# A decoder layer on one core: which engine makes a weight block's low part, where the gates' exponentials stay, and how the compression's places are read

## The chip, the core and the metric

The kernel runs on one core of a Trainium2 chip. The metric is the device time of one execution in microseconds (us), the median of the runs shown. The engines run side by side, each through its own queue of instructions in a fixed order, and wait for one another by semaphores: TensorE (PE) for matmuls, VectorE (DVE), ScalarE (ACT) and GpSimd (POOL) for elementwise work, SyncE (SP) for starting transfers from memory.

## The reference, cut to what matters

One layer: a convolution module and a sparse attention with three branches stand side by side, are gated and projected; then cross-attention; then a feed-forward block. x is 256 tokens by 1024. Three places of it are touched by the change:

```
z = blocks + pos;  z = einsum("bnlgd,lde->bnge", z, w1);  k_cmp = silu(z) @ w2     # 15 blocks of 32 tokens, 4 groups
g = sigmoid(gate_logits)                       # 256 tokens x 3 branches x 16 heads
o = g[0] * o_cmp + g[1] * o_slc + g[2] * o_win
y = sigmoid(g_conv) * conv_out + sigmoid(g_attn) * nsa_out     # g_attn = h @ 1024 columns of w_in
```

All is float32. A softmax follows each branch's scores, so a branch gate can be multiplied into its softmax's divisor.

## The kernel before, in words

**Split products.** A product of float32 matrices is made as three fast products: each operand is split into a rounded high part and a low part, the rest. `split` makes the two parts of a weight: ACT copies to the high part (L177), and a subtraction makes the low part (L179), on POOL for the blocks in the list `aside`, on DVE for all others. A block holds 256 columns of a weight and comes in two halves of 128x1024 values; `ga2_0` is the first half of the block ga2, `ga2_0h` and `ga2_0l` its parts. PE then makes high times high, high times low, low times high (L246).

**The blocks' order and buffers.** `CHUNKS` lists the blocks: ... vs, vw, ga0 to ga3 (the attention gate's logits), gc0 to gc3 (the convolution gate's), and so on. Before the change `aside` runs from u1 to ga1, so the low parts of ga0 and ga1 are made on POOL, those of ga2, ga3 and all later blocks on DVE. A half is loaded by SP (L210) into one of four buffers (tag "w"), free again when its low part is made; the high and low parts have five buffers each. The framework's scheduler plays the program against modelled times, fixes each engine's order by it and hands out each buffer that it holds to be free first; which load follows which subtraction is therefore part of the built program.

**The convolution's taps.** 31 taps per channel block are added up: on DVE by multiply-adds that accumulate in PSUM (`taps_v`, L422; the last of a chain writes to `yt`), and for the first block in part by ACT products (vw, L431) that POOL adds one after another to `yt` (`taps_g`, L434). Each of POOL's additions needs the result of the one before.

**The attention's start.** `compressed_scores` has PE make the compressed branch's scores into two banks (cs_ps0, cs_ps1); DVE adds them to the bias in `nsc` (L698). A first bank of tag "s" (two banks in all) is free for another use when that is done. The raw branch gates are transposed by PE to `gt_ps`, in the only bank of tag "s0". ACT writes exp(-g) of them to `sgt` in SBUF (L715), and DVE makes from that twice 1 + exp(-g) in two instructions, `igc` and `igd` (L718), which later divide the softmaxes. Then come the scores of the first pair of heads: `s1` (L735), one bank of tag "s" per head, and `s0` (L737) in the bank that gt_ps had. So the second s1 waits for nsc, and s0 for what reads gt_ps last. `between` makes the products of ga2, ga3, gc0 and so on in pieces between the pairs of heads.

**The compression.** `hidden` multiplies the gathered places of keys and values (`kvt`, per place 4 groups and one more for the position, each of 16) by `w1t` in 32 matmuls. Each reads 5 rows of 15 places, 75 columns with a step from row to row.

Of the kernel before, what the change touches and what calls it, by code (L numbers as in the profile page):

```python
# [11 lines left out]
AF = mybir.ActivationFunctionType  # L12
ALU = mybir.AluOpType
AX = mybir.AxisListType

P = 128
# [4 lines left out]
GROUPS = 4  # L21
HD = 64
# [8 lines left out]
NCMP = 15  # L31
# [4 lines left out]
CHUNKS = (  # L36
    [f"k{j}" for j in range(1, 4)] + [f"u{j}" for j in range(8)]
    + ["kc", "vc"] + [f"q{j}" for j in range(4)] + ["ks", "kw", "vs", "vw"]
    + [f"ga{j}" for j in range(4)] + [f"gc{j}" for j in range(4)]
    + [f"pw{j}" for j in range(4)] + [f"wo{j}" for j in range(4)]  # L40
    + [f"xq{j}" for j in range(4)] + [f"v{j}" for j in range(4)]
    + [f"xo{j}" for j in range(4)] + [f"f{j}" for j in range(NF)]
)
CHUNK_AT = {n: i for i, n in enumerate(CHUNKS)}
# [53 lines left out]
def tile_hybrid_block(  # L98
# [16 lines left out]
    nc = tc.nc  # L115
# [6 lines left out]
    def long(name, slot, shape=(P, NB, S), dt=F32):  # L122

        return sb.tile(list(shape), dt, tag=f"L{slot}", name=name)
# [9 lines left out]
    def small(name, shape, dt=F32, tag=None, bufs=1):  # L134
        if len(shape) == 2 and shape[1] < LINE:
            return sb.tile([P, LINE], dt, tag=tag or name, name=name, bufs=bufs)[:, 0:shape[1]]
        return sb.tile(shape, dt, tag=tag or name, name=name, bufs=bufs)
# [10 lines left out]
    def aux(name, shape, tag, bufs):  # L148
        return axp.tile(shape, F32, tag=tag, name=name, bufs=bufs)
# [31 lines left out]


    first, splits = {}, {}
    aside = CHUNKS[CHUNK_AT["u1"]:CHUNK_AT["ga2"]]

    def behind(*marks):

        stack = ExitStack()
        for m in marks:
            stack.enter_context(tc.issue_after(m.ins))  # L190
        return stack
# [40 lines left out]
    def in_line():  # L232
        return behind(*last)
# [153 lines left out]
    for i in range(4):  # L387
        hs = slice(2 * i, 2 * i + 2)
        for kb in (2 * i, 2 * i + 1):
            vec = nc.vector.scalar_tensor_tensor(out=hf[:, kb], in0=xt_t[:, kb], scalar=col(PP_GMIX, kb),  # L390
                                                 in1=r1, op0=ALU.mult, op1=ALU.mult)
# [62 lines left out]
    for j in range(NB):  # L454
        ps = gemm(f"u{j}", h)
        sg = small(f"sg{j}", [P, S], tag="sg", bufs=3)
# [9 lines left out]
    with behind(loads["u6_1"]):  # L466
# [5 lines left out]
                     start=True, stop=True)  # L472
    cb_ps = aux("cb_ps", [P, 2, 16, HEADS], "o", 1)
    for qb in range(2):
        for i, ns in enumerate(CGROUPS):
            n0, n1 = ns[0], ns[-1] + 1
            mm = nc.tensor.matmul(cb_ps[:, qb, n0:n1].rearrange("p n h -> p (n h)"), lhsT=cbt[:, i, qb * P:qb * P + P],
                                  rhs=relt[:, RT_CB + 16 * n0:RT_CB + 16 * n1], start=True, stop=True)
# [21 lines left out]
    kvt = [long(f"{n}t", slot, (P, 8, GROUPS + 1, 16)) for n, slot in (("k", 11), ("v", 13))]  # L500
    for kv, name in enumerate(("kc", "vc")):
        ps = gemm(name, h)
        kc = kvt[kv]
        for g in range(2):
            for odd in range(2):
                at = ps[HD * g:HD * g + HD].rearrange("p b (m l o) -> p b l m o", l=8, o=2)[:, :, :, :, odd]
# [10 lines left out]
    def hidden():  # L517


        z_ps = aux("z_ps", [P, GROUPS + 1, NCMP], "o", 1)  # L520
        with in_line():
            for l in range(16):
                for kv in range(2):
                    mm = nc.tensor.matmul(z_ps[HD * kv:HD * kv + HD], lhsT=w1t[:, kv, l],
                                          rhs=kvt[kv][:, l % 8, :, l // 8:l // 8 + NCMP], start=l == 0, stop=l == 15)
        last[:] = [mm]
        zs = small("zs", [P, GROUPS, NCMP], tag="zs", bufs=2)
        at = small("at", [P, 1])
        nc.scalar.activation(at, z_ps[:, GROUPS, 0:1], AF.Copy)
        sig = nc.scalar.activation(zs, z_ps[:, :GROUPS], AF.Sigmoid, bias=at)  # L530

        with behind(sig):
            nc.scalar.activation(small("exps", [P, 1]), eps1, AF.Exp)
        z1 = zz[:HD, 0, :64].rearrange("p (g n) -> p g n", g=GROUPS)[:, :, 0:NCMP]
        nc.vector.scalar_tensor_tensor(out=z1, in0=z_ps[:HD, :GROUPS], scalar=at[:HD], in1=zs[:HD], op0=ALU.add, op1=ALU.mult)
        nc.vector.scalar_tensor_tensor(out=zs[HD:], in0=z_ps[HD:, :GROUPS], scalar=at[HD:], in1=zs[HD:], op0=ALU.add, op1=ALU.mult)
        nc.scalar.activation(zz[HD:, 1].rearrange("p (g r n) -> p g r n", g=GROUPS, r=4)[:, :, :, 0:NCMP],
                             zs[HD:].unsqueeze(2).to_broadcast([HD, GROUPS, 4, NCMP]), AF.Copy)

# [17 lines left out]
    for j in range(4):  # L557
        ps = gemm(f"q{j}", h)
        q0, q1 = (qt[j // 2][:, 4 * (j % 2) + k:4 * (j % 2) + k + 3:2] for k in range(2))
        nc.scalar.activation(q0[0:64], ps[0:64], AF.Copy, scale=-0.125)  # L560
        act = nc.scalar.activation(q1[64:128], ps[64:128], AF.Copy, scale=-0.125)
        nc.vector.scalar_tensor_tensor(out=q0[64:128], in0=ps[0:64], scalar=-0.125, in1=f(q0[0:64]),
                                       op0=ALU.mult, op1=ALU.subtract)
        vec = nc.vector.scalar_tensor_tensor(out=q1[0:64], in0=ps[64:128], scalar=-0.125, in1=f(q1[64:128]),
                                             op0=ALU.mult, op1=ALU.subtract)
        convolve(11, (1, 0, 1, 1)[j], act, vec)
        if j == 1:
            hidden()
# [28 lines left out]
    ng = 3 * HEADS  # L597
# [9 lines left out]
    with in_line():  # L607
        for n, x in enumerate(h):
            for kb in range(NB):
                mm = nc.tensor.matmul(g_ps, lhsT=wgs[:, kb].rearrange("p c n -> p (c n)"), rhs=x[:, kb],  # L610
                                      start=n + kb == 0, stop=n * kb == NB - 1)
# [64 lines left out]
    with behind(splits["ga0_1"][1]):  # L676
        for c in range(2):
            for i in range(2):
                nc.gpsimd.tensor_tensor(out=vcm[:, c, 8 * i:8 * i + 8], in0=f(vcs[:, c, i]).unsqueeze(1).to_broadcast([P, 8, HD]),
                                        in1=hm, op=ALU.mult)  # L680
# [28 lines left out]
    gt_ps = aux("gt_ps", [P, 2, ng], "s0", 1)  # L709
# [1 line left out]
    for tb in range(2):  # L711
        nc.tensor.matmul(gt_ps[:, tb], lhsT=sgn[:, tb * P:tb * P + P], rhs=cpt[:, CP_GS:CP_GS + ng], start=tb == 0, stop=tb == 1)

    sgt = small("sgt", [P, 2, ng], tag="sg", bufs=3)
    nc.scalar.activation(sgt, gt_ps, AF.Exp, scale=-1.0)  # L715
    for to, g in ((igc, sgt[:, :, 0:HEADS]), (igd.rearrange("p h t b -> p t b h"),
                                              sgt[:, :, HEADS:3 * HEADS].rearrange("p t (b h) -> p t b h", b=2))):
# [6 lines left out]
    def scores(hp):  # L724

        g = hp // 2
        nbp = bias_of(hp)
        s0 = aux(f"s0_{hp}", [P, 2, 2, P], "s0", 1)
        p0 = small(f"p0_{hp}", [P, 2, 2, P], tag="p0", bufs=2)
        p1 = []  # L730
        for k, hd in enumerate(heads_of(hp)):
            s1 = aux(f"s1_{hd}", [P, 2, S], "s", 2)
            with in_line():
                for i, t in enumerate((kdh, kdl)):
                    nc.tensor.matmul(s1, lhsT=qh(hd, 1), rhs=t[:, g].rearrange("p b t -> p (b t)"), start=i == 0, stop=i == 1)  # L735
                for i, t in enumerate((kdh, kdl)):
                    mm = nc.tensor.matmul(s0[:, k], lhsT=qh(hd, 0), rhs=t[:, g, :, 0:P], start=i == 0, stop=i == 1)  # L737
            p1.append(small(f"p1_{hd}", [P, 2, S], tag="pr", bufs=4))
            for br in range(2):
                nc.vector.tensor_tensor_reduce(out=p1[k][:, br], in0=s1[:, br], in1=nbp[:, k], scale=1.0, scalar=3e38,  # L740
                                               op0=ALU.add, op1=ALU.min, accum_out=mins[:, hd, 1, br:br + 1])
        last[:] = [mm]
        for k, hd in enumerate(heads_of(hp)):
            for br in range(2):
                least = nc.vector.tensor_tensor_reduce(out=p0[:, k, br], in0=s0[:, k, br], in1=nbp[:, k, P:S], scale=1.0, scalar=3e38,
                                               op0=ALU.add, op1=ALU.min, accum_out=mins[:, hd, 0, br:br + 1])
        first["scores"] = least,
        return p0, p1
# [86 lines left out]
    p = [scores(0)]  # L835
# [462 lines left out]
    u1, u25, u3, u35 = more = [small(f"more{n}", [P, 512], tag="vt", bufs=4) for n in range(4)]  # L1298
# [187 lines left out]
```

## Time and profile before

| what | value |
|---|---|
| median of the runs shown | 539.82 us (3 runs, 539.81 to 545.05) |
| profiled execution, its own time | 542.99 us |
| span in its trace, first to last instruction | 540.7 us |
| mean granted TensorE clock | 0.992 |

The trace is of one execution with the profiler on; times in it count from the span's start. In its rows the engine stands before line, operation, out<-in and shape; tile names are without their numbers, so ga_0l can be the first half's low part of any of the four blocks. An idle time before an instruction stands in brackets with what ended it.

### The profile page before, as it was taken

The page shows a single profiled execution, that of the slowest core. Times are in us where ns is not written, and L with a number is a line of the kernel's source. Part 1 is how long each engine was busy: PE and PEld are TensorE (multiplying, and loading weights), DVE is VectorE, ACT ScalarE, POOL GpSimd, SP SyncE. Part 2 cuts the span into 40 slices and gives each one's busy share as a digit, 9 for nine tenths or more (in the row PEclk, how much of TensorE's full clock was granted, in tenths as well). Part 3 has the DMA queues.
Part 4 walks back from the last instruction along what each step waited for, and adds up shares of the span by engine and source line. Part 5 has one row for each costly group of instructions (what it writes and reads, how often), then busy time and mean ns, then how long its engine had stood idle before and what let it go on. Part 6 is the DMA issues. An engine that isn't in the chain of part 4 may idle for free.

```text
span 540.7 us, 10518 instructions
## 1 busy us (share of the span) xinstructions
PE 529.8 (98%) x3963; PEld 495.4 (92%) x3963; DVE 455.0 (84%) x913; ACT 357.6 (66%) x649; POOL 155.7 (29%) x109
## 2 busy tenths in 40 slices
PE   9999999999979999999999999999999999999995
PEld 8999999999969988999999999988888888888884
DVE  4868899899989898885869676588899999879996
ACT  4675475787674887969547755576676677648563
POOL 0079999899971000301003100150000000000001
PEclk9999999999979999999999999999999999999999
DMA  8927954665153744438655742757846668438632
GB/s 323 402 83 233 369 180 162 208 195 161 62 183 126 223 151 135 135 98 233 205 198 170 270 138 98 220 171 205 261 158 193 198 208 237 159 121 245 198 118 78
DMA packets 30739, 101.52 MB, mean 188 GB/s; under 512 B 3296, under 2 KB 5856, under 8 KB 30304
## 3 DMA queue, kind: packets, MB, share of 16 engines
q1 hardware_dynamic: 29104, 96.99, 53.8%
q0 software_dynamic: 864, 2.62, 2.8%
q10 hardware_dynamic: 720, 1.23, 0.6%
q8 instruction: 31, 0.51, 0.4%
q14 instruction: 20, 0.16, 0.1%
HBM read 99.59 MB, written 1.25 MB: 186 GB/s over the span
## 4 chain that ended last, share of the span: by engine, by line
PE 60%; DVE 1%; ACT 0%; issue 0%; ACTq 0%; DVEq 0%
PE ps_f L1203 15%; PE ps_f L1205 7%; PE fo L1242 6%; PE ps_xo L246 4%; PE ps_v L246 4%; PE ps_pw L246 4%; PE ps_wo L246 4%; PE ps_xq L246 4%; PE m L1242 4%; PE xo_ps L970 1%; PE xs L970 1%; PE o L801 1%; PE pt_a L780 1%; PE s L735 1%; PE o L798 1%; PE pt_b L780 0%
## 5 line engine op out<-in xcount | busy, mean ns | idle before, releaser
L422 DVE SCALAR_TENSOR_TENSOR yp<-vt,ppt,yp 128x256 f32<-128x256 f32 x196 | 78.4, 486 | 0.2
L1203 PE MATMUL ps_f<-g,f_1h 128*128 128x512 f32 x176 | 49.0, 397 | 0.0
L1203 PE MATMUL ps_f<-g,f_0h 128*128 128x512 f32 x176 | 48.3, 396 | 0.0
L1203 PEld LDWEIGHTS ps_f<-g,f_1h 128*128 128x128 f32 x176 | 32.9, 188 | 7.6
L1203 PEld LDWEIGHTS ps_f<-g,f_0h 128*128 128x128 f32 x176 | 29.9, 188 | 4.0
L179 DVE TENSOR_TENSOR f_1l<-f,f_1h 128x1024 fp32r<-128x1024 f32 x22 | 27.4, 1248 | 5.0 <-ACT f_1h L177 4.1
L1205 PEld LDWEIGHTS ps_f<-g,f_0l 128*128 128x128 f32 x176 | 26.8, 188 | 3.9
L179 DVE TENSOR_TENSOR f_0l<-f,f_0h 128x1024 fp32r<-128x1024 f32 x22 | 26.8, 1219 | 1.8 <-ACT f_0h L177 1.7
L177 ACT ACTIVATE f_1h<-f 128x1024 fp32r<-128x1024 f32 x22 | 23.2, 1056 | 7.0 <-PE ps_xo L246 3.7
L1205 PE MATMUL ps_f<-g,f_0l 128*128 128x256 f32 x176 | 27.4, 277 | 0.0
L179 POOL TENSOR_TENSOR u_0l<-u,u_0h 128x1024 fp32r<-128x1024 f32 x7 | 17.3, 2469 | 31.7 <-ACT u_0h L177 31.7
L434 POOL TENSOR_TENSOR yt<-yt,vw 128x512 f32<-128x512 f32 x17 | 25.2, 1482 | 3.0 <-ACT vw L431 2.7
L1205 PE MATMUL ps_f<-g,f_1l 128*128 128x256 f32 x176 | 25.8, 277 | 0.0
L177 ACT ACTIVATE f_0h<-f 128x1024 fp32r<-128x1024 f32 x22 | 23.1, 1050 | 2.7 <-DMA f<-in_wst_dram 1.3
L1206 ACT ACTIVATE ab<-ps_f 128x256 f32<-128x256 f32 x44 | 16.5, 375 | 11.6 <-PE ps_f L1205 10.9
L755 ACT ACTIVATE p<-p,mins 128x256 f32<-128x256 f32 x32 | 15.9, 503 | 10.3 <-DVE mins L740 10.3
L1205 PEld LDWEIGHTS ps_f<-g,f_1l 128*128 128x128 f32 x176 | 22.6, 188 | 0.0
L1119 POOL DMA_DIRECT2D spare<-in_wfo_dram x1 | 0.9, 866 | 74.2 <-DVE ab L1207 74.2
L1207 DVE TENSOR_TENSOR ab<-ps_f,ab 128x256 f32<-128x256 f32 x44 | 18.3, 419 | 3.0 <-ACT ab L1206 2.8
L290 ACT ACTIVATE uh<-sl 128x256 fp32r<-128x256 f32 x22 | 9.1, 414 | 14.0 <-DVE sl L1211 14.0
L179 POOL TENSOR_TENSOR u_1l<-u,u_1h 128x1024 fp32r<-128x1024 f32 x7 | 17.9, 2552 | 0.0
L310 POOL TENSOR_TENSOR nt_l<-nr_l 128x2 f32<-128x2 f32 x4 | 1.0, 241 | 55.0 <-DVE nr_l L307 54.7
(658 smaller groups left out, 1701.0 us busy)
## 6 DMA issues: line engine op xcount, KB each, us to landing
f<-in_wst_dram SPq DMA_DIRECT2D x44, 512.0 KB, 5.5
fo<-in_wfo_dram SPq DMA_DIRECT2D x16, 512.0 KB, 3.9
u<-in_wst_dram SPq DMA_DIRECT2D x14, 512.0 KB, 8.3
q<-in_wst_dram SPq DMA_DIRECT2D x8, 512.0 KB, 4.5
ga<-in_wst_dram SPq DMA_DIRECT2D x8, 512.0 KB, 4.1
gc<-in_wst_dram SPq DMA_DIRECT2D x8, 512.0 KB, 3.7
v<-in_wst_dram SPq DMA_DIRECT2D x8, 512.0 KB, 6.6
pw<-in_wst_dram SPq DMA_DIRECT2D x8, 512.0 KB, 5.8
```

The costliest lines, as they stand in the source:

```text
L177: copy = nc.scalar.activation(hi, w, AF.Copy)
L179: splits[name] = copy, eng.tensor_tensor(out=lo, in0=w, in1=f(hi[:]), op=ALU.subtract)
L246: mm = nc.tensor.matmul(ps[:, b], lhsT=lhsT, rhs=rhs, start=row + b + kb == 0, stop=kb == NB - 1 and row == 2 and b == 1)
L422: nc.vector.scalar_tensor_tensor(out=out[:, i] if t == ts[-1] else acc[i], in0=v, scalar=w, in1=acc[i], op0=ALU.mult, op1=ALU.add)
L434: nc.gpsimd.tensor_tensor(out=yt[:, 0:2], in0=yt[:, 0:2], in1=pr, op=ALU.add)
L755: exp.append(nc.scalar.activation(p1[k][:, br], p1[k][:, br], AF.Exp, scale=-1.0, bias=mins[:, hd, 1, br:br + 1], accum_out=sums[:, hd, 1, ...
L970: mm = nc.tensor.matmul(o, lhsT=lhsT, rhs=rhs, start=n == 0, stop=n == len(order) - 1)
L1203: nc.tensor.matmul(ps, lhsT=hs[kb // 4][0][:, kb % 4, cs], rhs=fg[:, :, kb], start=kb == 0, stop=False)
L1205: nc.tensor.matmul(ps[:, 1], lhsT=hs[kb // 4][1][:, kb % 4, cs], rhs=fg[:, 0, kb], start=False, stop=kb == NB - 1)
L1206: nc.scalar.activation(ab[:, b], ps[:, 0], AF.Copy)
L1207: joins[b] = nc.vector.tensor_tensor(out=ab[:, b], in0=ps[:, 1], in1=ab[:, b], op=ALU.add)
L1242: mm = nc.tensor.matmul(o, lhsT=a[x], rhs=b[w], start=start and n == 0, stop=stop and n == 2)
```

## The change

Three edits. The list `aside` ends one block later, so the low parts of ga2 are made on POOL. The compression's matmuls read 65 neighbouring places in place of 75 in rows: 4 groups of 16, of which 15 are used, and one place of the position's row. ACT writes the gates' exponentials back to gt_ps in PSUM and igc and igd read them there, so s0, which takes that bank, now comes after igc and igd.

```diff
-    aside = CHUNKS[CHUNK_AT["u1"]:CHUNK_AT["ga2"]]
+    aside = CHUNKS[CHUNK_AT["u1"]:CHUNK_AT["ga3"]]
...
-        z_ps = aux("z_ps", [P, GROUPS + 1, NCMP], "o", 1)
+        z_ps = aux("z_ps", [P, 16 * GROUPS + 1], "o", 1)
         with in_line():
             for l in range(16):
                 for kv in range(2):
                     mm = nc.tensor.matmul(z_ps[HD * kv:HD * kv + HD], lhsT=w1t[:, kv, l],
-                                          rhs=kvt[kv][:, l % 8, :, l // 8:l // 8 + NCMP], start=l == 0, stop=l == 15)
+                                          rhs=kvt[kv][:, l % 8].rearrange("p g n -> p (g n)")[:, l // 8:l // 8 + 16 * GROUPS + 1],
+                                          start=l == 0, stop=l == 15)
         last[:] = [mm]
+        z_at = z_ps[:, 16 * GROUPS:]
+        z_ps = z_ps[:, 0:16 * GROUPS].rearrange("p (g n) -> p g n", g=GROUPS)[:, :, 0:NCMP]
         zs = small("zs", [P, GROUPS, NCMP], tag="zs", bufs=2)
         at = small("at", [P, 1])
-        nc.scalar.activation(at, z_ps[:, GROUPS, 0:1], AF.Copy)
-        sig = nc.scalar.activation(zs, z_ps[:, :GROUPS], AF.Sigmoid, bias=at)
+        nc.scalar.activation(at, z_at, AF.Copy)
+        sig = nc.scalar.activation(zs, z_ps, AF.Sigmoid, bias=at)
...
-    sgt = small("sgt", [P, 2, ng], tag="sg", bufs=3)
+    sgt = gt_ps
     nc.scalar.activation(sgt, gt_ps, AF.Exp, scale=-1.0)
```

The edits move instructions, since the scheduler sets the order anew. Below the second edit, line numbers of the changed kernel are three higher than before. On POOL, ga2_0l and ga2_1l now stand between the first and the second of the six additions L434 that follow ga1_1l; nothing else moves there. On PE the order is unchanged. Three queues, with buffer numbers kept in the names:

On DVE, around the first scores, before the change. nsc is the compressed scores' addition; the taps end with the two rows that write yt; ga2_0l stands fifteen taps ahead of nsc:

```order
L422 SCALAR_TENSOR_TENSOR yt_354<-vt3_347,ppt_66,yp7_1450 128x256
L698 TENSOR_TENSOR nsc_989<-cs_ps0_2000,nsc_989 128x256 x2
L179 TENSOR_TENSOR ga2_1l_2188<-ga2_1_2185,ga2_1h_2187 128x1024
L179 TENSOR_TENSOR ga3_0l_2220<-ga3_0_2217,ga3_0h_2219 128x1024
L718 TENSOR_SCALAR igc_1911<-sgt_2082 128x32
L718 TENSOR_SCALAR igd_1910<-sgt_2082 128x4x16
L740 ISA p1_0_2098,mins_1984<-s1_0_2093,nb0_2088 128x256
```

And after the change at the same place (the rows left out are the rest of the first pair's s1):

```order
L422 SCALAR_TENSOR_TENSOR yt_354<-vt3_347,ppt_66,yp7_1450 128x256
L179 TENSOR_TENSOR ga3_0l_2219<-ga3_0_2216,ga3_0h_2218 128x1024
L701 TENSOR_TENSOR nsc_989<-cs_ps0_2000,nsc_989 128x256 x2
L743 ISA p1_0_2097,mins_1984<-s1_0_2092,nb0_2087 128x256
...
L721 TENSOR_SCALAR igc_1911<-gt_ps_2079 128x32
L721 TENSOR_SCALAR igd_1910<-gt_ps_2079 128x4x16
L748 ISA p0_0_2091,mins_1984<-s0_0_2090,nb0_2087 128x128
```

ga2's two low parts have left, ga3_0l stands ahead of nsc where it stood behind, and igc and igd stand behind the first pair's s1.

On ACT, from the high part of ga2's second half to the gates' exponential, before the change; sga is the tanh of a ga block's product, vw the taps' products:

```order
L177 ACTIVATE ga2_1h_2187<-ga2_1_2185 128x1024
L177 ACTIVATE ga3_0h_2219<-ga3_0_2217 128x1024
L662 ACTIVATE sga_1913<-ps_ga0_1916 128x512
L431 ACTIVATE vw16_1878<-vt0_344,ppt_66 128x256 x2
L177 ACTIVATE ga3_1h_2249<-ga3_1_2247 128x1024
L431 ACTIVATE vw17_1882<-vt0_344,ppt_66 128x256 x2
L177 ACTIVATE gc0_0h_2308<-gc0_0_2306 128x1024
L662 ACTIVATE sga_1913<-ps_ga1_1985 128x512
L715 ACTIVATE sgt_2082<-gt_ps_2079 128x96
```

And after it:

```order
L177 ACTIVATE ga2_1h_2186<-ga2_1_2184 128x1024
L177 ACTIVATE ga3_0h_2218<-ga3_0_2216 128x1024
L665 ACTIVATE sga_1913<-ps_ga0_1916 128x512
L431 ACTIVATE vw16_1878<-vt0_344,ppt_66 128x256 x2
L177 ACTIVATE ga3_1h_2248<-ga3_1_2246 128x1024
L177 ACTIVATE gc0_0h_2307<-gc0_0_2305 128x1024
L665 ACTIVATE sga_1913<-ps_ga1_1985 128x512
L431 ACTIVATE vw17_1882<-vt0_344,ppt_66 128x256 x2
L718 ACTIVATE gt_ps_2079<-gt_ps_2079 128x96
```

The products vw17 have moved behind gc0_0h and the tanh; gc0_0h stands ahead of the exponential in both.

On SP, the loads of the same blocks with the semaphores that each waits for (DVE_49 and Pool_49 count finished instructions of DVE and POOL, the others tell of earlier transfers), before the change:

```order
L210 DMA ga2_1_2185<-in_wst_dram 128x1024 [waits DMAHW0_49,Pool_49]
L210 DMA ga3_0_2217<-in_wst_dram 128x1024 [waits DMAHW5_49,DMAHW3_49,DVE_49]
L210 DMA ga3_1_2247<-in_wst_dram 128x1024 [waits DMAHW1_49,Pool_49]
L210 DMA gc0_0_2306<-in_wst_dram 128x1024 [waits DMAHW2_49,Pool_49]
L210 DMA gc0_1_2336<-in_wst_dram 128x1024 [waits DMAHW4_49,DVE_49]
```

And after it:

```order
L210 DMA ga2_1_2184<-in_wst_dram 128x1024 [waits DMAHW0_49,Pool_49]
L210 DMA ga3_0_2216<-in_wst_dram 128x1024 [waits DMAHW1_49,DMAHW5_49,Activation_49,Pool_49]
L210 DMA ga3_1_2246<-in_wst_dram 128x1024 [waits DMAHW2_49,Pool_49]
L210 DMA gc0_0_2305<-in_wst_dram 128x1024 [waits DMAHW5_49,DVE_49]
L210 DMA gc0_1_2335<-in_wst_dram 128x1024 [waits DMAHW3_49,Pool_49]
```

Before, ga3_0 followed the low part ga2_0l on DVE, and ga3_1 and gc0_0 followed ga1_0l and ga1_1l on POOL. Now ga3_0 and ga3_1 follow ga1_0l and ga1_1l, gc0_0 follows ga3_0l on DVE, and gc0_1 ga2_0l on POOL.

More of the change, by code (lines that the diff above doesn't have):

```diff
@@ L534, in hidden @@
         z1 = zz[:HD, 0, :64].rearrange("p (g n) -> p g n", g=GROUPS)[:, :, 0:NCMP]
-        nc.vector.scalar_tensor_tensor(out=z1, in0=z_ps[:HD, :GROUPS], scalar=at[:HD], in1=zs[:HD], op0=ALU.add, op1=ALU.mult)
-        nc.vector.scalar_tensor_tensor(out=zs[HD:], in0=z_ps[HD:, :GROUPS], scalar=at[HD:], in1=zs[HD:], op0=ALU.add, op1=ALU.mult)
+        nc.vector.scalar_tensor_tensor(out=z1, in0=z_ps[:HD], scalar=at[:HD], in1=zs[:HD], op0=ALU.add, op1=ALU.mult)
+        nc.vector.scalar_tensor_tensor(out=zs[HD:], in0=z_ps[HD:], scalar=at[HD:], in1=zs[HD:], op0=ALU.add, op1=ALU.mult)
         nc.scalar.activation(zz[HD:, 1].rearrange("p (g r n) -> p g r n", g=GROUPS, r=4)[:, :, :, 0:NCMP],
```

## The prediction

> **What bounds the kernel now.** I read the head of the page, then the waits of TensorE (PE), then the timeline and the table by stretches around its two long waits.
>
> ```profile
> span 540.7 us, 10518 instructions
> PE 529.8 (98%) x3963; PEld 495.4 (92%) x3963; DVE 455.0 (84%) x913; ACT 357.6 (66%) x649; POOL 155.7 (29%) x109
> ```
>
> PE works through 98% of the span, so only its own work and its few pauses count. The two longest rows of its waits (who waits, for whom, us in total, times, longest):
>
> ```profile
> PE s L735 <- DVE nsc L698: 2.0, 1, 2.0
> PE s L737 <- ACT sgt L715: 1.8, 1, 1.8
> ```
>
> Both lie at the first scores of the attention. PE's timeline there (start, duration, instruction, idle time before it):
>
> ```profile
> 150.76 0.40 PE L735 MATMUL s<-kdl,qt 128*128 128x512 f32 x1
> 153.17 0.77 PE L735 MATMUL s<-kdh,qt 128*128 128x512 f32 x1 [2.01 <-DVE nsc L698]
> 156.15 0.58 PE L737 MATMUL s<-kdh,qt 128*128 128x256 f32 x1 [1.79 <-ACT sgt L715]
> 157.17 1.91 PE L246 MATMUL ps_ga<-hh,ga_0h 128*128 128x256 f32 x8
> 161.11 0.36 PE L246 MATMUL ps_ga<-hh,ga_0l 128*128 128x256 f32 x1
> ```
>
> The table by stretches (stretch, its length, PE busy, granted clock, DMA share and rate):
>
> ```profile
> 149.70:153.10 3.40, 1.46 (x11) 1.00 0.71 290
> 153.10:156.50 3.40, 1.55 (x3) 0.50 0.33 101
> 156.50:159.90 3.40, 3.40 (x17) 0.50 0.56 210
> 159.90:163.30 3.40, 3.40 (x30) 1.00 0.24 77
> ```
>
> The clock is halved for 6.8 us behind the first pause; 4.95 us of work run in them, so 2.5 us are lost. Pauses and clock cost 6.3 us together. This is the most that the change could win, and from here on PE runs without a long wait, so whatever arrives later than 156.15 moves the end.
>
> Why PE waits is seen on VectorE (DVE). The trace leaves block numbers out of names: the row at 138.30 is ga2_0l, the first half of the third block, and 152.94 is its second, ga2_1l.
>
> ```profile
> 138.30 8.05 DVE L179 TENSOR_TENSOR ga_0l<-ga,ga_0h 128x1024 fp32r<-128x1024 f32 x1
> 146.28 5.18 DVE L422 SCALAR_TENSOR_TENSOR yp<-vt,ppt,yp 128x256 f32<-128x256 f32 x13
> 152.15 0.87 DVE L698 TENSOR_TENSOR nsc<-cs_ps,nsc 128x256 f32<-128x256 f32 x2
> 152.94 1.22 DVE L179 TENSOR_TENSOR ga_1l<-ga,ga_1h 128x1024 fp32r<-128x1024 f32 x1
> 156.29 1.25 DVE L718 TENSOR_SCALAR igc<-sgt 128x32 f32<-128x32 f32 x1
> 157.46 0.21 DVE L718 TENSOR_SCALAR igd<-sgt 128x64 f32<-128x64 f32 x1
> ```
>
> A low part takes 1.22 us on DVE (152.94), but ga2_0l took 8.05. GpSimd's (POOL's) rows over the same time:
>
> ```profile
> 137.20 2.46 POOL L179 TENSOR_TENSOR ga_0l<-ga,ga_0h 128x1024 fp32r<-128x1024 f32 x1
> 139.56 2.11 POOL L679 TENSOR_TENSOR vcm<-vcs,cpt 128x512 fp32r<-128x512 f32 x2
> 141.57 2.46 POOL L179 TENSOR_TENSOR ga_1l<-ga,ga_1h 128x1024 fp32r<-128x1024 f32 x1
> 143.92 1.35 POOL L434 TENSOR_TENSOR yt<-yt,vw 128x512 f32<-128x512 f32 x1
> 145.35 2.14 POOL L434 TENSOR_TENSOR yt<-yt,vw 128x512 f32<-128x512 f32 x1
> 147.57 1.28 POOL L434 TENSOR_TENSOR yt<-yt,vw 128x512 f32<-128x512 f32 x1
> ```
>
> POOL's instructions up to 143.92 overlap: each starts about 0.1 us before its predecessor ends. The first gap is behind the addition that ends at 143.92 + 1.35 = 145.27, since the next addition needs its result. DVE ends at 146.35, 1.08 later, and the addition at 145.35 takes 2.14 in place of 1.28. So I read: a subtraction with both inputs in SBUF is shut out while POOL's instructions follow each other closely, and gets in at a gap.
>
> **The change, part by part.** *65 columns.* One of the two groups of matmuls, which run side by side (busy us, mean ns, idle before):
>
> ```profile
> L524 PE MATMUL z_ps<-kt,w1t 128*64 128x75 f32 x32 | 2.3, 230 | 0.0
> ```
>
> If columns set the pace, 65/75 of 2.3 us saves 0.3; if weight loads do, 0. I take 0.3, and nothing of it at the end: it only brings PE 0.3 earlier to a pause that DVE ends.
>
> *Third block on POOL.* POOL's order becomes: addition at 143.92, ga2_0l, ga2_1l, addition, then the others. The two low parts need nothing that is not there, and the addition behind them needs only the one at 143.92. So there is no gap: at 2.36 per low part (141.57 to 143.92) and 1.26 for an addition in close order (1.35 less the overlap) they start at 145.18 and 147.54, the addition at 149.90, and the first gap is at 149.90 + 1.35 = 151.25. PE needs ga2_0l at 161.11 in the trace; 147.6 is early enough.
>
> On DVE the 8.05 go, and the fifteen taps run from 138.30 for 5.87 (146.28 to 152.15) to 144.2. Next in its row is now **ga3_0l, ahead of nsc**. Its data come by 145.2, by the page's median for such a load and the row of ScalarE (ACT) in front of its high part:
>
> ```profile
> ga<-in_wst_dram SPq DMA_DIRECT2D x8, 512.0 KB, 4.1
> 143.12 1.06 ACT L177 ACTIVATE ga_1h<-ga 128x1024 fp32r<-128x1024 f32 x1
> ```
>
> The load follows ga1_0l (137.20 + 2.46 = 139.66) and lands by 143.8; ACT is free at 144.2 and takes 1.0. So ga3_0l arrives while POOL's row is close, and is let in at 151.25; with the 1.08 above it ends at 152.33. nsc follows at 152.25 and PE's second score at 153.27, against 153.17 now. The shut-out has only changed its victim.
>
> *What is queued behind it.* The load of gc0_0 takes the buffer that ga3_0l frees, and on ACT gc0_0h now stands ahead of the gates' exponential. The comparable load was ga3_0, which waited for ga2_0l (end 146.35):
>
> ```profile
> 146.38 0.80 SPq L210 DMA_DIRECT2D ga<-in_wst_dram  x2
> 150.45 1.06 ACT L177 ACTIVATE ga_0h<-ga 128x1024 fp32r<-128x1024 f32 x1 [6.27 <-DMA ga<-in_wst_dram]
> 151.41 0.58 ACT L662 ACTIVATE sga<-ps_ga 128x512 f32<-128x512 f32 x1
> 151.89 0.90 ACT L431 ACTIVATE vw<-vt,ppt 128x256 f32<-128x256 f32 x2
> 152.69 1.05 ACT L177 ACTIVATE ga_1h<-ga 128x1024 fp32r<-128x1024 f32 x1
> 155.86 0.24 ACT L715 ACTIVATE sgt<-gt_ps 128x96 f32<-128x96 f32 x1
> ```
>
> Issue to use took 4.07. So gc0_0 is issued at 152.36 and gc0_0h starts at 156.43. Behind it stand one tanh and two vw products, as behind ga3_0h (152.69 - 150.45 = 2.24), then the exponential: 158.67 to 158.91. vw's buffer needs POOL's addition of 151.25 and is free by then. Behind the exponential, ACT holds those of the first scores, which PE needs only when it transposes them, after the products of ga2, ga3 and most of gc0.
>
> *Exponentials left in PSUM.* PE's next score (s0) waited for the exponential; now it also waits for igc and igd, which read that bank. No row shows them on PSUM: igd's 0.21 is one bound, igc's 1.25, behind an addition on POOL, the other. I take 0.21 each. The Trainium skill (VectorE: DVE Perf Modes, Why PSUM operands drop a tier) says that a PSUM operand rules out the mode that reads through both SBUF ports; if that mode is what made igc wait for POOL, the page gives the sum as taken, and the row of 1.25 one that is 1.0 higher. s0 starts at 158.91 + 0.42 + 0.15 (nsc's end at 153.02 to 153.17) = 159.48: **3.33 us later** than 156.15.
>
> *Clock.* PE then pauses over 5 us, so it restarts at half clock. Above, it got full clock after one 3.4 us stretch full of work; counted from the restart that is 3.4 to 6.8 us, a loss of 1.7 to 3.4. The trace loses (159.9 - 156.15)/2 = 1.9 behind s0. Difference -0.2 to +1.5; I take +0.65. The Trainium skill (TensorE: Matmul & The Clock Gate, HAM oscillation) puts the limit at idle gaps over about 3.4 us. Here pauses of 2.01 and 1.79 were enough, so the measurement decides. By the page only the changed kernel would lose clock, 2.55 in the middle, and the sum would be 5.9.
>
> Sum: 3.33 + 0.65 = +4.0. The profiled execution took 542.99 for its span of 540.7, so 547.0 there; on the median of 539.82 it is **543.8**. With a landing 0.4 shorter, or igc 1.0 longer, and the clock's ends: 542.5 to 545.9.
>
> **Rivals.** *DVE is let in early (faster).* One earlier case speaks for it:
>
> ```profile
> 30.95 2.82 POOL L179 TENSOR_TENSOR u_0l<-u,u_0h 128x1024 fp32r<-128x1024 f32 x1 [30.50 <-ACT u_0h L177]
> 32.02 2.84 DVE L179 TENSOR_TENSOR u_1l<-u0w,u_1h 128x1024 fp32r<-128x1024 f32 x1
> 33.74 3.38 POOL L179 TENSOR_TENSOR u_1l<-u,u_1h 128x1024 fp32r<-128x1024 f32 x1
> ```
>
> There POOL's second instruction started 0.03 before the first ended, and DVE got in all the same. Against it: the overlap at 137 to 144 is 0.1, and four changes of instruction passed DVE by (139.56 to 143.92, with one between the two vcm). Let in at 145.27, ga3_0l ends at 146.35, gc0_0h starts at 150.45, nsc makes nobody wait; vw then waits for POOL's addition (151.25 + 0.85 of delay), and s0 starts at 152.1 + 0.8 + 0.24 + 0.42 + 0.15 = 153.7, 2.4 early. With +0.65 of clock or, if the one pause of 2.5 halves nothing, -1.9: -1.8 to -4.3, **537**. Let in one instruction later, all is 2.4 later: about 540. The case decides by the first DVE low part: under 2.5 us there.
>
> *The load lands late (slower by over 1%).* The page's medians by tile:
>
> ```profile
> gc<-in_wst_dram SPq DMA_DIRECT2D x8, 512.0 KB, 3.7
> v<-in_wst_dram SPq DMA_DIRECT2D x8, 512.0 KB, 6.6
> ```
>
> gc0_0 sits on the path alone with ACT waiting for it. At 6.6 in place of 4.07 the sum is +6.5: **546.3**; it passes 1% from 5.5 on. For it: two further loads are issued right behind. Against: so they were at 146.38, and that took 4.07.
>
> *The columns change nothing*: the same 543.8, since the 0.3 is hidden.
>
> **How the numbers follow.** 1% is 5.4 us, about what a measurement of this kernel can tell from no change. Forecast 0.66; let in early 0.25 (0.16 at the first change, 0.09 later); late load 0.09. Slower by over 1% is the late load and a little of the forecast's upper end: 0.11. Faster by over 1% would need nearly the whole 6.3: 0.02. Within 1%: 0.87. The range runs from 537.0, the middle of the early case, to 545.5, the forecast's upper end less its tail, and leaves about 2 in 10 out. The forecast's own is 542.5 to 545.9.
>
> **What would show it.** In the changed profile: a DVE low part that starts near 145 and takes about 7 us; POOL's two low parts around 145 and 147.5; PE's waits on nsc of about 2.4 and on igd of about 5; ACT idle for about 7 us before gc0_0h, ended by a DMA; clock 0.5 for 6.8 us or more. A DVE low part under 2.5 us there, or an exponential before 156, would make the forecast wrong.

## The result and the profile after the change

The changed kernel took 545.44 us (median of 16 runs, 543.91 to 546.95), the kernel before 541.29 beside it (median of 16 runs, 539.00 to 545.05): ratio 1.0076, 95% interval 1.0056 to 1.0096, so 3.0 to 5.2 us slower and 4.15 by the medians. The forecast was 4.0 slower. Its absolute 543.8 stood on a median of 539.82 of three runs, which sixteen runs put 1.5 higher. For that reason 545.44 lies only 0.06 inside the upper end of the stated range, 545.5.

In the table of PE's waits the two longest have changed places: the one at s0 has grown from 1.8 to 5.0, the one for nsc is there still (who waits, for whom, us in total, times, longest). The name behind the first is of no use; by the program s0 waits for igd, which ends 0.15 before s0 starts.

```profile
PE s L740 <- ACT p L758: 5.0, 1, 5.0
PE s L738 <- DVE nsc L701: 1.8, 1, 1.8
```

PE's timeline after the change (start, duration, instruction, idle time before it) shows the second score and then s0:

```profile
148.53 0.40 PE L738 MATMUL s<-kdl,qt 128*128 128x512 f32 x1
150.74 0.72 PE L738 MATMUL s<-kdh,qt 128*128 128x512 f32 x1 [1.81 <-DVE nsc L701]
...
156.84 0.55 PE L740 MATMUL s<-kdh,qt 128*128 128x256 f32 x1 [4.95 <-ACT p L758]
```

All of this lies some 2.4 us earlier than in the profile before: PE got its full clock 2.3 us sooner (4.02 against 6.32), which is worth 1.1, and went through the same matmuls between 101 and 128 in 1.0 us less (the last section comes back to this). One execution stands against one here, so the spans alone (542.3 against 540.7) tell little; I compare from a common point, the start of ga1_0l on POOL, which is 134.76 now and was 137.20: 2.44 apart. DVE:

```profile
142.22 7.58 DVE L179 TENSOR_TENSOR ga_0l<-ga,ga_0h 128x1024 fp32r<-128x1024 f32 x1
149.72 0.87 DVE L701 TENSOR_TENSOR nsc<-cs_ps,nsc 128x256 f32<-128x256 f32 x2
...
156.32 0.19 DVE L721 TENSOR_SCALAR igc<-gt_ps 128x32 f32<-128x32 f32 x1 [3.62 <-ACT gt_ps L718]
156.43 0.26 DVE L721 TENSOR_SCALAR igd<-gt_ps 128x64 f32<-128x64 f32 x1
```

The first row is ga3_0l, shut out for 7.58 us, with nsc right behind it. POOL meanwhile makes ga2_1l and the first of the additions, which ends at 148.72:

```profile
145.08 2.41 POOL L179 TENSOR_TENSOR ga_1l<-ga,ga_1h 128x1024 fp32r<-128x1024 f32 x1
147.44 1.28 POOL L434 TENSOR_TENSOR yt<-yt,vw 128x512 f32<-128x512 f32 x1
```

SP's queue and ACT show the rest of the chain. The load of gc0_0 goes out when ga3_0l has ended (149.80):

```profile
149.83 0.33 SPq L210 DMA_DIRECT2D gc<-in_wst_dram  x1
```

ACT waits 7.58 us for it, with the tanh, the two vw products and the exponential behind:

```profile
145.17 1.06 ACT L177 ACTIVATE ga_1h<-ga 128x1024 fp32r<-128x1024 f32 x1 [1.43 <-PE cs_ps L698]
153.81 1.06 ACT L177 ACTIVATE gc_0h<-gc 128x1024 fp32r<-128x1024 f32 x1 [7.58 <-DMA gc<-in_wst_dram]
154.78 0.58 ACT L665 ACTIVATE sga<-ps_ga 128x512 f32<-128x512 f32 x1
155.25 0.90 ACT L431 ACTIVATE vw<-vt,ppt 128x256 f32<-128x256 f32 x2
156.05 0.24 ACT L718 ACTIVATE gt_ps<-gt_ps 128x96 f32<-128x96 f32 x1
```

The clock by stretches (stretch, its length, PE busy, granted clock, DMA share and rate) is halved for 10.24 us in place of 6.83:

```profile
147.38:150.79 3.41, 1.60 (x13) 1.00 0.00 0
150.79:161.03 10.24, 5.29 (x21) 0.50 0.48 163
161.03:164.44 3.41, 3.41 (x31) 1.00 0.15 53
```

### The profile page after: what moved, and what is told of

It is laid out like the page before. It is cut to its first block, busy times and chain, and to the rows that moved or that the text cites. A ratio compares the mean times of both kernels' runs of the same rounds, so it can differ in the third digit from the quotient of the medians.

```text
span 542.3 us, 10521 instructions
## 1 busy us (share of the span) xinstructions
PE 527.6 (97%) x3963; PEld 493.4 (91%) x3963; DVE 449.7 (83%) x911; ACT 358.0 (66%) x649; POOL 158.4 (29%) x111
## 3 DMA queue, kind: packets, MB, share of 16 engines
HBM read 99.59 MB, written 1.25 MB: 186 GB/s over the span
## 4 chain that ended last, share of the span: by engine, by line
PE 60%; DVE 1%; ACT 0%; issue 0%; ACTq 0%; DVEq 0%
PE ps_f L1206 15%; PE ps_f L1208 7%; PE fo L1245 6%; PE ps_xo L246 4%; PE ps_v L246 4%; PE ps_pw L246 4%; PE ps_wo L246 4%; PE ps_xq L246 4%; PE m L1245 4%; PE xo_ps L973 1%; PE xs L973 1%; PE o L804 1%; PE pt_a L783 1%; PE s L738 1%; PE o L801 1%; PE pt_b L783 0%
## 5 line engine op out<-in xcount | busy, mean ns | idle before, releaser
L434 POOL TENSOR_TENSOR yt<-yt,vw 128x512 f32<-128x512 f32 x17 | 22.9, 1345 | 2.9 <-ACT gt_ps L718 2.7
```

The source lines that it names most:

```text
L434: nc.gpsimd.tensor_tensor(out=yt[:, 0:2], in0=yt[:, 0:2], in1=pr, op=ALU.add)
```

## The experiments

The theory has two links: DVE's low part is shut out until POOL's row has a gap, and gc0_0's load, which waits for that low part, holds ACT's exponential and with it s0. All kernels were timed against the kernel before, in two groups on one chip each, whose medians of before were 542.36 and 541.69. The ratios below come with 95% intervals and are not the quotients of the medians (for the longer row 549.15 over 541.69 would be 1.0138).

**The first edit alone.**

```diff
-    aside = CHUNKS[CHUNK_AT["u1"]:CHUNK_AT["ga2"]]
+    aside = CHUNKS[CHUNK_AT["u1"]:CHUNK_AT["ga3"]]
```

> Only the first edit is made (ga2's low parts on POOL); the columns and the gates' exponentials are as before. Theory: the low part ga3_0l still stands ahead of nsc on DVE and the load of gc0_0 still follows it, so nearly the whole loss is here: a DVE low part of 7 to 8 us, PE's wait on nsc about 1.8, its wait for the exponential about 4.5 (0.45 shorter than in the changed kernel, since igc and igd no longer stand between), and 3.7 us over the kernel before, 545.0 or ratio 1.007. Rival (the exponentials in PSUM make the loss): no difference from before, ratio 1.000, and an exponential before 156. Rival (the columns hide a gain): ratio over 1.008.

Measured: 545.57 us, ratio 1.0055 (1.0027 to 1.0082). Nearly the whole loss is in this edit. From ga1_0l on POOL (137.26) to s0 (158.91) pass 21.65 us, against 18.95 before the change and 22.08 with all three edits; so the first edit costs 2.70 of the 3.13, and igc and igd on the way to s0 the other 0.43. Two numbers were missed: there is no wait for nsc, and s0's wait is 4.96 in place of 4.5. In the table of PE's waits only s0's is long.

```profile
PE s L737 <- ACT sgt L715: 5.0, 1, 5.0
```

In this execution PE fell 2.3 us behind the trace of before in the first 80 us (last section) and came to the second score just as nsc ended. POOL's row was not later than in that trace (ga1_0l at 137.26 against 137.20), so a pause that POOL and DVE set absorbed what PE had lost ahead of it.

**The other two edits alone.**

```diff
-    aside = CHUNKS[CHUNK_AT["u1"]:CHUNK_AT["ga3"]]
+    aside = CHUNKS[CHUNK_AT["u1"]:CHUNK_AT["ga2"]]
```

(against the changed kernel)

> The second and third edits alone (65 columns, the gates' exponentials in PSUM); ga2's low parts stay on DVE as before the change. Theory: the columns save about 0.2 us of PE ahead of a pause that DVE ends, so nothing at the end; igc and igd on PSUM now stand between the exponential and s0 and cost 0.4: ratio 1.001. Rival (the columns' gain reaches the end): 0.999. Rival (the PSUM edit makes a large part of the loss): over 1.004.

Measured: 542.79 us, ratio 1.0007 (0.9980 to 1.0035), as the theory had it; the interval takes in the second expectation too, so only the third falls.

**nsc ahead of ga3_0l.** Against the changed kernel:

```diff
-            first[("ga2_1", "ga3_1")[qb]] = added,
+            first[("ga3_0", "ga3_1")[qb]] = added,
```

> The changed kernel with one order more: ga3_0's split stands behind nsc. On DVE nsc then precedes ga3_0l; the buffers are handed out anew by it, so gc0_0's load follows ga2_0l on POOL (end about 145.1) in place of ga3_0l on DVE. Theory: nsc runs as soon as the compressed scores are there, about 145.2, and PE does not wait for it; ga3_0l is shut out until about 149.7 all the same; gc0_0 lands about 149.2, the exponential is at about 151.6, igc and igd by 152.2, so PE has one pause of about 2.5 us and s0 starts at about 152.3 in place of 156.84. With a clock loss between none and 3 us: 538.5 to 541.5, middle 540.3, ratio 0.998. Rival (the shut-out is not due to POOL's close row but to ga3_0l's own data): ga3_0l takes under 2.5 us here. Rival (only the pause on nsc matters, the load does not): 1.8 us less than the changed kernel, 543.6.

Measured: 541.14 us, ratio 0.9973 (0.9952 to 0.9994). The wait for nsc is gone, and ga3_0l is shut out all the same, for as long as POOL's row lasts from its start, so that its own data held it falls:

```profile
145.51 0.88 DVE L701 TENSOR_TENSOR nsc<-cs_ps,nsc 128x256 f32<-128x256 f32 x2 [2.56 <-PE cs_ps L698]
146.31 4.84 DVE L179 TENSOR_TENSOR ga_0l<-ga,ga_0h 128x1024 fp32r<-128x1024 f32 x1
```

s0 starts at 153.10; measured from POOL's ga1_0l it was expected at 153.66 of this trace, and is 5.1 us earlier than with the change. PE's one pause is 3.38 in place of 2.5. The expectation that only the pause on nsc matters (543.6) falls.

**The exponential ahead of gc0_0's high part.** Against the changed kernel:

```diff
-    nc.scalar.activation(sgt, gt_ps, AF.Exp, scale=-1.0)
+    first["gc0_0"] = nc.scalar.activation(sgt, gt_ps, AF.Exp, scale=-1.0),
```

> The changed kernel with one order more: gc0_0's high part stands behind the gates' exponential on ACT; every other queue is as in the changed kernel. Theory: ga3_0l is shut out for 7 to 8 us and PE waits 1.8 for nsc as in the changed kernel, gc0_0's load comes as late, but the exponential no longer waits for it: it runs at about 149.6 to 150.5, igc and igd follow the first pair's minima at about 152.7, and s0 starts at about 153.1 in place of 156.84. PE has two pauses of 1.8 and 1.4, as before the change: 541.4, ratio 1.000. Rival (the landing is not what holds the exponential, but igc and igd or POOL's additions): s0 stays within 0.5 of 156.8 and the time at 545.

Measured: 541.34 us, ratio 0.9976 (0.9951 to 1.0000). On DVE, POOL and SP the order is that of the changed kernel, ga3_0l takes 7.62, and the load comes as late. PE's waits:

```profile
PE s L738 <- DVE nsc L701: 2.5, 1, 2.5
PE s L740 <- DVE igd L721: 1.2, 1, 1.2
```

So the landing was what held the exponential: with that queue crossed, s0's wait falls from 4.95 to 1.24. The clock took its part back:

```profile
153.20:163.44 10.24, 9.06 (x42) 0.50 0.48 168
```

Half of 9.06, 4.5 us, is lost here, against 2.5 before the change, though both kernels pause for 3.7 to 3.8 us in two pieces.

**Both orders.** The two edits above together.

> The changed kernel with both orders (nsc ahead of ga3_0l on DVE, the gates' exponential ahead of gc0_0's high part on ACT). Theory: no wait for nsc; ga3_0l is shut out until about 149.7 and stands ahead of the first pair's minima, these end about 151.2, igc and igd by 151.6, so PE has one pause of about 1.8 and s0 starts at about 151.7. If one such pause still halves the clock for 6.8 us: 540.4; if it does not: 537.4, ratio 0.993. Rival (what was won here is given back at a later load or low part): the two waits go and the time stays above 541.

Measured: 540.25 us, ratio 0.9974 (0.9945 to 1.0003), with one wait left, and the clock halved behind it:

```profile
PE s L740 <- DVE igd L721: 3.0, 1, 3.0
...
PE o L801 <- ACT ptt_b L786: 0.6, 1, 0.6
```

```profile
153.59:157.00 3.41, 3.41 (x18) 0.50 0.30 104
```

igd is late because the first scores' minima stand behind ga3_0l, which ends at 151.58. The stretch of half clock was half as long as expected, and the pause 1.2 longer, so the expected 540.4 was met by two misses that offset each other.

**POOL's row made longer.** Against the changed kernel, ga2_1l is made twice on POOL, the second time behind the addition that follows; the order of every other queue is unchanged:

```diff
-            splits[name] = copy, eng.tensor_tensor(out=lo, in0=w, in1=f(hi[:]), op=ALU.subtract)
+            splits[name] = [(copy, eng.tensor_tensor(out=lo, in0=w, in1=f(hi[:]), op=ALU.subtract)) for _ in range(1 + (name == "ga2_1"))][-1]
```

> The changed kernel with one POOL instruction more: the low part ga2_1l is made a second time, behind the addition that follows it, so that POOL's close row is longer by one low part and one addition, 2.35 + 1.25 = 3.6 us. Every other queue is in the same order. Theory (a subtraction of DVE with both inputs in SBUF gets in at the first gap of POOL's row and ends 1.05 to 1.08 us behind it): ga3_0l takes about 11.2 us in place of 7.58; PE's wait on nsc is about 5.4 in place of 1.8; gc0_0's load, its high part, the exponential and s0 all come 3.6 later; 549.0 us (548.0 to 550.0 with the clock), ratio about 1.014. Rival (DVE is let in when POOL leaves its low parts for the additions): ga3_0l takes 7.6 as in the changed kernel and the time is 545.4.

Measured: 549.15 us, ratio 1.0110 (1.0077 to 1.0144). The expected 549.0 is met, the expected 1.014 lies at the upper end of the interval. ga3_0l on DVE:

```profile
143.86 10.75 DVE L179 TENSOR_TENSOR ga_0l<-ga,ga_0h 128x1024 fp32r<-128x1024 f32 x1 [0.98 <-ACT ga_0h L177]
```

On POOL the second ga2_1l and the addition behind it, which ends at 153.52:

```profile
149.93 2.38 POOL L179 TENSOR_TENSOR ga_1l<-ga,ga_1h 128x1024 fp32r<-128x1024 f32 x1
152.22 1.30 POOL L434 TENSOR_TENSOR yt<-yt,vw 128x512 f32<-128x512 f32 x1
```

DVE was passed by all of POOL's instructions that followed, the first addition among them, and ended at 154.61. From POOL's ga1_0l (136.07) s0 (161.54) is 3.39 later than with the change. PE's wait for nsc is 6.60 where 5.4 was expected, since PE came to it sooner in this execution. That DVE is let in when POOL leaves its low parts falls.

**The gap made earlier.** Against the changed kernel, ga2_1l is ordered behind two additions; "lows" holds marks for low parts alone and "adds" the additions L434:

```diff
+            with behind(*lows.get(name, ())): splits[name] = copy, eng.tensor_tensor(out=lo, in0=w, in1=f(hi[:]), op=ALU.subtract)
...
-    gate(1, few)
+    gate(1, few); lows["ga2_1"] = adds[13],
```

> The changed kernel with POOL's low part ga2_1l put behind two additions, which depend on each other, so that POOL's row has its first gap one low part earlier. The order follows it: nsc stands ahead of ga3_0l on DVE, igc and igd ahead of the second of the first scores' minima, vw17 ahead of gc0_0's high part. To be read against the kernel in which only nsc is put first, where ga3_0l starts at 146.3 too and took 4.84 us. Theory: ga3_0l ends 1.07 behind the earlier gap, after about 2.4 us. Rival (DVE is let in when POOL's two low parts are done): 4.8 us or more. The time, by either, about 540.5, since nsc and the load no longer wait for ga3_0l.

One run, 543.53 us. ga3_0l on DVE:

```profile
146.73 2.83 DVE L179 TENSOR_TENSOR ga_0l<-ga,ga_0h 128x1024 fp32r<-128x1024 f32 x1
```

POOL's addition ahead of the gap ends at 148.48:

```profile
147.18 1.30 POOL L434 TENSOR_TENSOR yt<-yt,vw 128x512 f32<-128x512 f32 x1
```

It takes 2.83 in place of 4.84, while ga2_1l is still to come, and ends at 149.56. The time is 3 us over the expectation. The clock is the larger part: it was halved for 10.24 us with PE busy for 9.57 of them, so 4.8 were lost, against 2.4 (half of 4.82) where only nsc was first. A single run says little on the time, though: those of the kernel before, without one outlier, lay between 538.40 and 545.71 in this group.

The first link in one table, over all traces with such a low part (worked out from the rows, us):

| kernel | POOL's first gap at | low part starts | takes | ends behind the gap |
|---|---|---|---|---|
| before (ga2_0l) | 145.27 | 138.30 | 8.05 | 1.08 |
| second and third edit alone (ga2_0l) | 143.11 | 135.94 | 8.26 | 1.09 |
| after (ga3_0l, as in all below) | 148.72 | 142.22 | 7.58 | 1.08 |
| first edit alone | 151.22 | 145.87 | 6.43 | 1.08 |
| exponential first | 150.42 | 143.88 | 7.62 | 1.08 |
| nsc first | 150.07 | 146.31 | 4.84 | 1.08 |
| both first | 150.51 | 147.00 | 4.58 | 1.07 |
| longer row | 153.52 | 143.86 | 10.75 | 1.09 |
| earlier gap | 148.48 | 146.73 | 2.83 | 1.08 |

In the trace's nanoseconds the last column is 1.081 to 1.086 throughout.

**A version that takes all waits away.** Against the changed kernel: the exponential ahead of gc0_0's high part, vw17 behind both, and ga3_0's low part behind igc and igd.

```diff
-        convolve(13 + NB * TAPS * br, 1 + TAPS * br, act, splits[name + "_1"][0])
+        convolve(13 + NB * TAPS * br, 1 + 4 * br, act, splits[name + "_1"][0])
...
-    nc.scalar.activation(sgt, gt_ps, AF.Exp, scale=-1.0)
+    first["gc0_0"] = nc.scalar.activation(sgt, gt_ps, AF.Exp, scale=-1.0),
+    convolve(0, 2, *first["gc0_0"])
...
-        nc.vector.tensor_scalar(out=to, in0=g, scalar1=2.0, scalar2=2.0, op0=ALU.mult, op1=ALU.add)
+        lows["ga3_0"] = nc.vector.tensor_scalar(out=to, in0=g, scalar1=2.0, scalar2=2.0, op0=ALU.mult, op1=ALU.add),
```

> The changed kernel with three orders: ga3_0's low part stands behind igc and igd on DVE, and on ACT the gates' exponential stands ahead of gc0_0's high part and of the taps' products vw17, which follow gc0_0's high part. Theory: nsc at about 146, the exponential as soon as the gates' product is there (149.3), igc and igd by 150.0, so PE reaches s0 at about 150.2 without a wait and the clock is not halved. Against the kernel with both orders (wait 2.98, half clock for 3.41 us with work throughout, 1.7 lost) 4.7 us less: 535.6, ratio to before about 0.989. Rival (the time is given back at a later wait, since ga3_0l and gc1_0's load come late): 539 to 541 with a new wait of PE of over 2 us behind s0.

Measured: 539.32 us, ratio 0.9948 (0.9921 to 0.9976): 0.2 to 0.8% faster than the kernel before, and so than the changed one. At the first scores all went as expected: the second score's last matmul and s0 follow each other, and the clock stays full.

```profile
149.49 0.40 PE L739 MATMUL s<-kdl,qt 128*128 128x512 f32 x1
149.77 0.35 PE L741 MATMUL s<-kdh,qt 128*128 128x256 f32 x1
```

But of the 4.7 us over the kernel with both orders little is left at the end: 0.9 by the medians, which come from two chips, 0.3 with each taken against its own chip's median of before, 1.4 by the ratios, whose intervals overlap. PE's waits between 160 and 190:

```profile
PE pt_b L784 <- DVE mins L749: 0.8, 1, 0.8
PE pt_a L784 <- DVE p L773: 0.7, 1, 0.7
PE pc_ps L886 <- DVE nsc L857: 0.3, 1, 0.3
```

No wait is over 2 us, yet the rival was nearer. Matmul by matmul, on the clock of the trace of before, PE's lead on that trace grows from 1.7 us ahead of the scores to 8.1 at 160. These 6.4 us are all of the 6.3 that the prediction named as the most to be won. Then the lead shrinks to 5.1 at 187, and the three waits are 1.8 of these 3.0. PE comes to the transposes of the probabilities sooner, and DVE does not deliver them sooner. Three of DVE's rows on the way there, first from the trace of before:

```profile
167.36 0.68 DVE L842 TENSOR_TENSOR nsc<-nsc,mc 128x512 f32<-128x512 f32 x1
167.96 0.15 DVE L762 SCALAR_TENSOR_TENSOR sums<-sums,igd 128x8 f32<-128x8 f32 x1
168.39 0.35 DVE L767 TENSOR_SCALAR p<-p,sums 128x256 f32<-128x256 f32 x1
```

And from this kernel's:

```profile
160.21 1.78 DVE L846 TENSOR_TENSOR nsc<-nsc,mc 128x512 f32<-128x512 f32 x1
161.91 1.26 DVE L766 SCALAR_TENSOR_TENSOR sums<-sums,igd 128x8 f32<-128x8 f32 x1
163.44 1.23 DVE L771 TENSOR_SCALAR p<-p,sums 128x256 f32<-128x256 f32 x1
```

With the row behind them (0.83 in place of 0.28) they take 3.6 us longer. Before, they came after POOL's last instruction of this part, which ended at 164.63; now they stand beside POOL's additions, and POOL goes on to 165.33. So the gain seems to go to the same two engines at the next place. No run moved these additions, so this is read from the trace and not tested.

## Why the prediction was right

Its times stand on the clock of the profile before; the changed trace is shifted by 2.44 for it (from ga1_0l on POOL).

| step | predicted | measured, shifted |
|---|---|---|
| POOL's first gap | 151.25 | 151.16 |
| ga3_0l ends | 152.33 | 152.24 |
| second score starts | 153.27 | 153.18 |
| gc0_0's load is issued | 152.36 | 152.27 |
| its high part starts | 156.43 | 156.25 |
| the exponential | 158.67 | 158.49 |
| s0 | 159.48 | 159.28 |
| s0 later by | 3.33 | 3.13 |
| clock behind s0 | +0.65 | +0.2 |

*65 columns.* From the first to the last of these matmuls 1.87 us pass, and 2.07 before: 0.2 of the 0.3 is there. PE then gained 1.0 more up to 128, which the prediction did not have (last section). At the end none of it shows: the second and third edits alone came to 1.0007, and the pause ends with nsc. The signs named 2.4 for PE's wait on nsc and it was 1.8; with the same order on DVE it was nothing with the first edit alone and 2.5 with the exponential first, since PE's place against POOL's row differs from execution to execution.

*Third block on POOL.* "The shut-out has only changed its victim" is what the trace shows, within 0.1 us. That a gap in POOL's row lets DVE in was read from one row; the nine traces of the table, with parts of 2.83 to 10.75 us, now give 1.07 to 1.09 from gap to end, and the two kernels that moved the gap moved the end with it. That a shared path into SBUF is behind it stays argued: no run shows the path. The Trainium skill (SBUF — State Buffer, Who interferes with whom) says that a DVE instruction with two SBUF inputs contends with a GpSimd one that reads SBUF, and that the order of issue decides who blocks. The kind agrees. By the same page of the Trainium skill (Summary: rules for kernel authors) the second one to issue blocks until the first finishes. Here the measurement decides: in the longer row DVE was passed by instructions that started up to 8.4 us after it (143.86, 152.22).

*What is queued behind it.* Issue to use took 3.98 (149.83 to 153.81) against 4.07. Putting the exponential first took s0's wait from 4.95 to 1.24 with the load as late as before, which shows the link.

*Exponentials left in PSUM.* igc and igd take 0.19 and 0.26 there, and from the exponential's end (156.29) to igd's it is 0.40; 0.42 was taken. The bound of 1.25 for igc, from an addition beside it, did not come, though one of POOL's additions ran here too (156.29 to 157.57).

*Clock.* This is the mis-sized term of the sum. Behind s0 the half clock lasts until 161.03, so (161.03 - 156.84)/2 = 2.1 us are lost there against 1.9: +0.2, inside the -0.2 to +1.5, where +0.65 was taken. In the trace the sum is thus 3.13 + 0.2 = 3.3. Matmul by matmul the changed kernel loses 3.1 us on the kernel before between 150 and 161 and nothing from there to the last matmul; behind that, its trace is 0.75 longer, with the cause open. So the agreement of 4.0 with the 4.15 of the medians is partly luck; the interval of 3.0 to 5.2 holds 3.3 and 4.0. The forecast's upper end of 545.9 is 0.2 above its own terms (539.82 + 3.33 + 1.0 + 1.5 = 545.65). On the limit for idle gaps that the Trainium skill gives (TensorE: Matmul & The Clock Gate, HAM oscillation; about 3.4 us), the runs go with the trace of before: one pause of 2.98 was enough (both first), and with none the clock stayed full (the last kernel).

*Rivals.* DVE was not let in early. In the case that spoke for it DVE ended 1.09 behind POOL's first instruction (34.86, 33.77), as behind a gap, though the second one overlapped by 0.03; it did so in all ten traces. The prediction's first reason against it, that the overlap at 137 to 144 is 0.1, fails: with the first edit alone and with the earlier gap DVE was passed by at overlaps of 0.03 too. What let it in at 33.77 is open. The late load did not come.

## What to carry to other kernels

A low part moved from DVE to POOL can shut out the next DVE instruction with two SBUF inputs for as long as POOL's instructions follow each other closely, here for up to 10.75 us: look in the new order for what stands there, and for the load and the queue behind it. A wait of PE that hangs on a transfer can be crossed by order alone: here each of two single reorderings won back the 4 us. And time won at a pause lasts only as far as the engines that feed the next meeting point come sooner too: of 6.4 us won there, the last kernel's trace kept 3.3.

## What the runs showed that was not expected

*Half clock comes in stretches of about 3.41 us*, one to four of them at the first scores (3.41, 6.83, 10.24 and 13.65 in these traces), and the sum of the pauses doesn't tell how many. Pauses of 3.7 to 3.8 us in two pieces cost 2.5 us once and 4.5 the other time. The traces show a grid behind it: in that of before, the clock is first full at 6.32 and first halved 146.77 us later, which is 43 steps of 3.413, and the other traces with a pause fit such steps too. In these nine the clock was halved at the end of the first step in which PE was busy for 0.43 to 2.04 us; a step with 2.37 in the last kernel left it full. In seven of them it came back at the end of the first step with PE busy for 3.19 us or more, and one step later with the exponential first and with the earlier gap; why is open. So it counts where in the grid a pause falls: one of 2.98 inside one step cost one stretch (both first), one of 3.38 across two steps cost two (nsc first). The grid starts elsewhere in each execution (first full clock between 4.02 and 6.81), so the +0.2 of the clock is the value of one execution.

*PE's pace differs by 3 to 4% at a granted clock of 1.00.* From 20 to 76 us of the first edit's trace, where PE was never idle, and then of the changed kernel's (the same matmuls but for a shift):

```profile
20.00:76.00 56.00, 56.00 (x476) 1.00 0.69 247
```

```profile
20.00:76.00 56.00, 56.00 (x493) 1.00 0.70 252
```

In the slow pace a matmul of 256 columns follows the one before by 118 ns, in the other by 113. It lasted from about 16 to about 80 us in the first edit's execution. From about 101 to 128, right behind the compression's matmuls, it shows in the two traces with 75 columns (before, first edit alone) and in none of the eight with 65, where PE gains 1.0 us. So this part may come from the second edit; one execution each does not show it. Whole microseconds between two profiles can come from such paces, so a common point near the change is better to compare from than the start, though it leaves out what an edit wins ahead of that point.
